# Spreading fourteen projection tiles over the Hyena transforms and moving the mLSTM branch behind them

## The chip, the cores and the metric

The kernel runs on one core of a Trainium2 chip. The metric is the device time of one execution in microseconds (us). The core's engines run their own instruction streams and wait for one another by semaphores: TensorE (PE) multiplies, ScalarE (ACT), VectorE (DVE) and GpSimd (POOL) work elementwise, and SyncE (SP) only issues transfers (DMA). The others issue transfers too, each in the queue of its own name.

## What is computed

One layer of a hybrid model: two token mixers side by side on the same normalised input, then a mixture of experts. 1,024 tokens (after 256 context tokens), width 1,024, fp32.

```
def token_mixer(h, w_in, b_in, ...):
    p = h @ w_in + b_in
    y_a = hyena_branch(p[..., :ML_START], ...)             # 3 x 512 columns
    y_b, state = mlstm_branch(p[..., ML_START:GATE_START], p[..., GATE_START:MERGE_START], ...)
    g_a, g_b = split(sigmoid(p[..., MERGE_START:]), 2)     # 2 x 1024 columns: the merge gates
    return (g_a * (y_a @ w_branch_hy) + g_b * (y_b @ w_branch_ml)) @ w_out, state

def hyena_branch(hy_p, ...):      # z <- x_n * (h_n conv z), twice, the convolution by FFT
    z = parts[0]
    for o in range(2):
        z = parts[o + 1] * bidir_long_conv(z, filt[:, o], skip[o])

def mlstm_branch(...):            # two scans over chunks of 128 tokens, one each way
    h = h2[:B] + flip(h2[B:])
    h = h * rsqrt(mean(h * h) + RMS_EPS) * norm_g          # per head
    return h * sigmoid(o)
```

After the mixers come a residual, a second norm, a router that lets each of 16 experts pick 128 tokens, the experts' SwiGLU, and the final norm.

## The kernel before

Every fp32 operand of a product is split in two parts (`split`: the high part `hi` by a cast on ACT, the low part `lo` by a subtraction on DVE or POOL), and a product is three matmuls (`mm3`: high by high, high by low, low by high). All engine calls go through one helper, so that the trace gives most instructions line 98; tiles are told apart by their names.

The stages, in order of time: the filters and the tokens' preparation with the first projections (to 336 us); the mLSTM stage (336 to 657 us); the head norm with more projection (657 to 797 us); the Hyena transforms (797 to 1008 us); the branch outputs, `w_out` and the router (to 1147 us); the choice of tokens (to 1212 us); the experts (to 2320 us).

**Projection.** `rest()` computes 32 tiles of 128 columns of `w_in` over all tokens (`hx`), each in two halves of 512 tokens of 24 matmuls: tiles j = 0 to 11 are Hyena's columns, 12 to 15 the mLSTM's output gate (to `o_d` in DRAM), 16 to 31 the merge gates (`gate_half`, a sigmoid, to `ga_d` and `gb_d` in DRAM). Weights come in blocks of 256 columns (`load_w`, `block`). A call of `rest_tile()` makes one tile in three substeps and, at its third, one step of `ada_rest` (the rest of the modulation, whose weights `wada` are loaded in blocks of 1 MB).

**mLSTM.** `mlstm()` runs two scans of ten chunks, forward and backward taking turns, each chunk (`ml_step`) in three substeps: 60 in all, one at each substep of 20 rest tiles. Within a step one chain goes through four engines: PE writes the log weights `pL` and the scores `pS`, ACT makes the exponentials `ae`, POOL masks them, DVE multiplies them by the scores (`ae<-ae,sc`), and PE needs the product for `pn<-v1c,ae`. The projection's matmuls (`ps<-hx,whi`, `ps<-hx,wlo`) stand between `pL` and `pn`.

**Head norm.** `head_norm()` norms the heads' outputs, transposes them on PE (`ps<-cst,hs`), multiplies by the output gate read from `o_d` and splits the result at once into `yb`, kept in SBUF. Eight more rest tiles stand between its parts, and the last four (`gate_tail`) behind them, with the loads of Hyena's tables (`hyena_pre`).

**Hyena.** There are four channel groups and two orders. `hyena_fwd(g, o)` has two steps (F = 0, 1): 24 matmuls `hyf<-D,hf` with 256 columns, then on DVE a chain `hX`, `hdf`, `hX`, `hY<-hX,Kt`, `hX<-hX,Kt`, `hY`, then on POOL `hY`, `hgd`, `hG`. The filters' spectra `Kt` are loaded from DRAM for each step, on SP's queue. `hyena_inv0` and `hyena_inv1` transform back, in fp32 (`hyE<-hG,hi`; with `hyE<-hi,hG` and `hyO<-hi,hG` for the second order). Between these steps `do` puts the units of `ml_branch`, the product of `yb` with `w_branch_ml` (`wmh`, `wml`): 16 units of 12 matmuls, each multiplied by a gate from `gb_d` (`mgb`). The last of all is `hyena_inv1(3)`, with the first half of four output products (`ps<-z,wb`) ahead of it.

**What sets the order.** A scheduler places the instructions of each engine, and on PE, ACT, DVE and POOL they need not stand in the order of the program. Small tiles of 2 KB a partition come from one pool of 12 buffers (`w2`); PSUM has eight banks.

Of the kernel before, what the change touches and what calls it, by code (L numbers as in the profile page):

```python
# [21 lines left out]
D = 1024  # L22
# [81 lines left out]
def layer_kernel(ctx: ExitStack, tc: tile.TileContext, A: dict, out: bass.AP, dbg=None, stop=None):  # L104
# [65 lines left out]
    o_d = dr.tile([512, 1024], F32, name="o_d")  # L170
    ga_d = dr.tile([1024, 1024], F32, name="ga_d")
# [509 lines left out]
    def to_chunks(dst_d, c0, j, cv, n_tok):  # L681
# [8 lines left out]
              + [[(3600 + 256 * b, 256)] for b in range(8)])  # L690
# [287 lines left out]

    def gate_half(w, j, n):
        dst, r0, c0 = (o_d, j - 12, c_bin + 24) if j < 16 else (ga_d, j - 16, c_bmg) if j < 24 else (gb_d, j - 24, c_bmg + 8)  # L980
        t = proj_half(w, j % 2, n * 512, col(c0 + r0))
        S.dma_start(dst[r0 * 128:(r0 + 1) * 128, n * 512:(n + 1) * 512], t)

    def rest():
        post = None
        for j in range(28):
# [63 lines left out]
    def rest_tile():  # L1050
        next(rs_)
        yield
        next(rs_)
        yield
        next(rs_, None)
        next(ar, None)
        yield


    yb = {}  # L1060

    def head_norm():
# [6 lines left out]
        yield  # L1069
        y0 = [al1([128, 4, 512], F32R, name="yb0", tag=t) for t in ("hch", "hcl")]  # L1070
        for n in range(2):
            pt = []
            for h in range(4):
                p = ps()
                for c in range(4):
                    T.transpose(p[:, c * 128:(c + 1) * 128], hsv(n * 4 + c)[:, h, :], ident)
                pt.append(p)
                if h % 2 == 1:
                    yield
            for h, p in enumerate(pt):  # L1080
                ot = w2([128, 512], name="ot")
                SY.dma_start(ot, o_d[h * 128:(h + 1) * 128, n * 512:(n + 1) * 512])
                V.scalar_tensor_tensor(ot, p, col(c_mng + h), ot, op0=OP.mult, op1=OP.mult)
                if n == 0:
                    hi, lo = y0[0][:, h], y0[1][:, h]
                else:
                    t = alx([128, 2, 512], F32R, name="yb1", tag="xt", bufs=4)
                    hi, lo = t[:, 0], t[:, 1]
                split(hi, lo, ot)
                yb[n, h] = hi, lo  # L1090
# [4 lines left out]
    for _ in range(20):  # L1095
        for _ in rest_tile():
            next(ml)
    if dbg is not None and "hs" in dbg:
        for i in range(4):
            SY.dma_start(dbg["hs"][:, 2 * i:2 * i + 2], hs[i])  # L1100
    hn = head_norm()
    for _ in range(8):
        for _ in rest_tile():
            next(hn, None)
    for _ in hn:
        pass
    for _ in ar:
        pass
    dump("eo", eo_d)
    mlp.close()  # L1110


    def gate_tail():
        for n in range(2):
            for j in range(28, 32):
                gate_half(block(6 + j // 2), j, n)
                yield
# [4 lines left out]
    n_D = [0]  # L1122

    def hyena_data():


        n_D[0] += 1
        al_, kw = (al, {"tag": "D2", "bufs": 2}) if n_D[0] % 3 == 0 else (alxl, {"tag": "xl", "bufs": 4})
        return tuple(al_([128, 4, 2, 128], F32R, name="D", **kw) for _ in range(2))
# [13 lines left out]
    def hyena_pre():  # L1143
        htab.append([al1([128, 2, 2, 4, 128], F32R, name=f"hf{v}", tag=f"hx0{v}", bufs=2) for v in range(2)])
        htab.append(al1([128, 2, 2, 4, 128], name="hi", tag="hx00", bufs=2))
        load_eo(0)
        for F in range(2):
            for c in range(2):
# [3 lines left out]
            if F == 0:  # L1152
                load_eo(1)
            yield
        SY.dma_start(htab[1], A["hi"])
# [17 lines left out]
    gt = gate_tail()  # L1173
    for _ in range(4):
        next(gt)
    run((hyena_pre(), 1), (gt, 1))
    p2.close()
    sx2.close()
    if stop == "mlstm":
        sxl.close()  # L1180
        sx1.close()
        sxt.close()
        return


    pz, p3 = ExitStack(), ExitStack()
    alz = phase(pz, "z")
    zs = {}
    al = phase(p3, "hyena")


    def ml_branch():
        ws = []

        def load():
            d_ = len(ws)
            raw = w2([128, 4, 128], name="wmr")
            S.dma_start(raw, A["w_branch_ml"][0][:, d_ * 128:(d_ + 1) * 128].rearrange("(k p) n -> p k n", p=128))
            w = [al([128, 4, 128], F32R, name=f"wm{v}", bufs=2) for v in "hl"]
            split(w[0], w[1], raw, G)  # L1200
# [3 lines left out]
        for d_, n in [(d_, n) for d_ in range(6) for n in range(2)] + [(d_, n) for n in range(2) for d_ in (6, 7)]:  # L1204
            yield
            if n == 0 and d_ < 7:
                load()
            sg = w2([128, 512], name="mgb")
            S.dma_start(sg, gb_d[d_ * 128:(d_ + 1) * 128, n * 512:(n + 1) * 512])
            p = ps()  # L1210
            for ct in range(4):
                mm3(p, [t[:, ct] for t in ws[d_]], yb[n, ct], ct == 0, ct == 3)
            V.tensor_tensor(sg, p, sg, op=OP.mult)
            SY.dma_start(mb_d[d_ * 128:(d_ + 1) * 128, n * 512:(n + 1) * 512], sg)
# [8 lines left out]
    def hyena_fwd(g, o):  # L1223
# [4 lines left out]
        if o == 0:  # L1228
            t = al([128, 4, 2, 128], name="hxe", tag="hx4", bufs=3)
            SY.dma_start(t.rearrange("p t x c -> p t (x c)"), eo_d[1, g].rearrange("t p x c -> p t (x c)"))  # L1230
        else:
            t = al([128, 1024], name="x2t", tag="hx4", bufs=3)
# [3 lines left out]
        for F in range(2):  # L1236
            Kt = al([128, 2, 2, 2, 128], name="Kt", bufs=3)
# [716 lines left out]
```

## Time and profile before

| what | us |
|---|---|
| median of three runs | 2340.99 (2339.63 to 2345.29) |
| the profiled execution, its own time | 2339.34 |
| its span in the profile | 2337.6 |
| PE busy in the span | 2183.2 |
| mLSTM stage, 336 to 657 | 321 |
| head norm, 657 to 797 | 140 |
| Hyena, 797 to 1008 | 211 |
| branch outputs, `w_out`, router, 1008 to 1147 | 139 |
| choice of tokens, 1147 to 1212 | 65 |
| experts, 1212 to 2320 | 1108 |

Read the stages first: an engine's busy time in a stage against the stage's length says which engine sets it. PE's clock is given as a share of full speed. Then come the waits of the engine that sets the stage, and last the instructions in order of time, where the length of a chain can be read off.

### The profile page before, as it was taken

The numbers are of one execution on the slowest core, as the hardware profiler recorded it, in microseconds if no ns is written. First come the engines' busy times: TensorE is split into PE (matmuls) and PEld (weight loads), VectorE is DVE, ScalarE is ACT, GpSimd is POOL, SyncE is SP. The second block draws the span as 40 slices with busy tenths as digits, with TensorE's granted clock in tenths as the row PEclk, the third lists the DMA queues.
The fourth block names the chain that finished last, engine by engine and source line by source line (L and its number), as shares of the span: only waits on it lengthen the run. The fifth ranks groups of instructions, "written<-read, shape, count | busy, mean of one in ns | idle before, by whom it ended". The sixth has DMA issues, their size and how long they took to land. (4 is left out here: it accounts for less than half of the span.)

```text
span 2337.6 us, 28219 instructions
## 1 busy us (share of the span) xinstructions
PE 2183.2 (93%) x10609; PEld 1777.0 (76%) x10609; DVE 1689.3 (72%) x1845; ACT 1244.1 (53%) x1388; POOL 447.2 (19%) x382
## 2 busy tenths in 40 slices
PE   6989999999999988799639999999999999999996
PEld 3679887787778777577538888888888888888884
DVE  4784445654341388963678889988898988888897
ACT  2441343334542211221427777787777777777774
POOL 3553101111100266532300110101111010111001
PEclk9879999999999989899869999999999999999998
DMA  7243335556533533384559999999999999999993
GB/s 260 91 139 91 120 113 164 202 171 216 171 113 101 159 112 125 113 265 167 184 213 367 384 382 379 389 385 377 387 385 380 379 391 381 379 389 382 380 348 147
DMA packets 227721, 600.97 MB, mean 257 GB/s; under 512 B 17307, under 2 KB 83927, under 8 KB 224385
## 3 DMA queue, kind: packets, MB, share of 16 engines
q1 hardware_dynamic: 203792, 543.05, 63.4%
q0 software_dynamic: 11488, 39.33, 5.4%
q10 hardware_dynamic: 12304, 16.80, 2.1%
q8 instruction: 83, 1.36, 0.2%
q14 instruction: 54, 0.43, 0.1%
HBM read 537.24 MB, written 61.88 MB: 256 GB/s over the span
## 5 line engine op out<-in xcount | busy, mean ns | idle before, releaser
L98 DVE TENSOR_TENSOR el<-er,eh 128x2048 fp32r<-128x2048 f32 x383 | 874.3, 2290 | 115.3 <-ACT eh L98 106.1
L98 ACT CAST eh<-er 128x2048 fp32r<-128x2048 f32 x384 | 733.6, 1915 | 236.8 <-PE pup L98 166.7
L98 PE MATMUL ps<-hx,whi 128*128 128x512 f32 x1280 | 404.5, 397 | 0.0
L98 PE MATMUL pup<-eh,xgh 128*128 128x512 f32 x1024 | 320.1, 394 | 1.6 <-ACT xgh L98 1.6
L98 PE MATMUL pup<-eh,xgl 128*128 128x512 f32 x1024 | 316.7, 390 | 0.0
L98 PEld LDWEIGHTS ps<-hx,whi 128*128 128x128 f32 x1280 | 237.9, 188 | 54.2 <-ACT nt L98 0.8
L98 PE MATMUL pup<-el,xgh 128*128 128x512 f32 x1024 | 274.3, 390 | 0.0
L98 PE MATMUL ps<-hx,wlo 128*128 128x512 f32 x640 | 252.5, 395 | 0.0
L98 PEld LDWEIGHTS pup<-eh,xgl 128*128 128x128 f32 x1024 | 192.9, 188 | 40.8 <-DVE xgl L98 0.2
L98 PEld LDWEIGHTS pup<-el,xgh 128*128 128x128 f32 x1024 | 192.5, 188 | 40.2
L98 PEld LDWEIGHTS pup<-eh,xgh 128*128 128x128 f32 x1024 | 190.4, 188 | 40.3 <-ACT xgh L98 2.0
L98 POOL DMA_INDIRECT acc_d<-ye,idxc x15 | 50.6, 3375 | 747.9 <-DVE ye L98 747.9
L98 PE MATMUL acc<-eh,gh 128*128 128x512 f32 x512 | 161.7, 397 | 0.2 <-ACT gh L98 0.2
L98 PE MATMUL acc<-eh,gl 128*128 128x512 f32 x512 | 160.3, 394 | 0.0
L98 PEld LDWEIGHTS ps<-hx,wlo 128*128 128x128 f32 x640 | 120.1, 188 | 28.2
L98 PE MATMUL acc<-el,gh 128*128 128x512 f32 x512 | 139.7, 394 | 0.0
L98 DVE TENSOR_TENSOR wlo<-wraw,whi 128x1024 fp32r<-128x1024 f32 (+1 forms) x44 | 55.8, 1271 | 100.4 <-ACT whi L98 93.8
L98 PEld LDWEIGHTS acc<-eh,gl 128*128 128x128 f32 x512 | 96.2, 188 | 22.8 <-DVE gl L98 0.4
L98 PEld LDWEIGHTS acc<-el,gh 128*128 128x128 f32 x512 | 96.1, 188 | 22.6
L98 PEld LDWEIGHTS acc<-eh,gh 128*128 128x128 f32 x512 | 95.0, 188 | 21.7 <-ACT gh L98 0.5
L98 ACT ACTIVATE pb<-ps,colv 128x512 f32<-128x512 f32 (+1 forms) x44 | 29.2, 665 | 130.1 <-PE ps L98 122.4
L98 ACT ACTIVATE sg<-ps,colv 128x512 f32<-128x512 f32 x40 | 27.5, 687 | 129.6 <-PE ps L98 123.2
(363 smaller groups left out, 3224.5 us busy)
## 6 DMA issues: line engine op xcount, KB each, us to landing
er<-in_w_exp_dram SPq DMA_DIRECT2D x384, 1024.0 KB
wada<-in_w_ada_dram SPq DMA_DIRECT2D x24, 1024.0 KB
wraw<-in_w_in_dram SPq DMA_DIRECT2D x40, 512.0 KB
K_d<-fk SPq DMA_DIRECT2D x32, 256.0 KB
Kt<-K_d SPq DMA_DIRECT2D x16, 512.0 KB
v1c<-v_d SPq DMA_DIRECT2D x20, 256.0 KB
eo_d<-eost POOLq DMA_DIRECT2D x16, 256.0 KB, 6.9
qc<-q_d SPq DMA_DIRECT2D x16, 256.0 KB
```

Of the source, the lines that this page charges most:

```text
L98: r = op(*a, **k)
```

## The change

- **Projection.** `rest()` stops after tile 17. The tiles j = 18 to 31 are made by a new generator `gate_tiles_T`: 28 steps, each half of the depth of one tile for all tokens (24 matmuls into a pair of PSUM banks `pg`), with weights `gwr` of 128 columns by 512 rows, loaded on SP's queue, cast on ACT (`gwh`), subtracted on DVE (`gwl`), three buffers each. `interleave` puts the 28 steps between 30 steps of Hyena.
- **mLSTM.** The same 60 substeps take 48 places of 16 rest tiles (`ml_steps`), and `ada_rest` does two of its steps per tile instead of one. The head norm has the last two rest tiles beside it, with the loads of Hyena's tables.
- **mLSTM output.** `head_norm` stores its product in `y_d` in DRAM (POOL's queue); `load_y` loads it again (`yr`) and splits it into `yb`. `ml_branch` stands behind the interleaved part, its units beside `hyena_inv1(2)` and `hyena_inv1(3)` and then beside `split_z` and the loads of `wb`. Its low part `wml` is made on DVE instead of POOL.
- **Hyena's buffers.** `Kt` has two instead of three, `hxe`/`x2t` two instead of three; `hY` gets two of its own (it shared four with `hX`); `hG` has none of its own, its values are written into `hX`. `z` is kept in fp32 (`z32`) and split later, and no output product starts before `hyena_inv1(3)`.

The core of the diff:

```diff
-              + [[(3600 + 256 * b, 256)] for b in range(8)])
+              + [[(3600, 256)]])
...
-        for j in range(28):
+        for j in range(18):
...
-        next(ar, None)
+        for _ in range(2):
+            next(ar, None)
...
+                V.scalar_tensor_tensor(ot, p, col(c_mng + h), ot, op0=OP.mult, op1=OP.mult)
+                G.dma_start(y_d[at], ot)
...
+    def ml_steps():
+        n = 0
+        for i in range(48):
+            yield
+            while n * 48 < (i + 1) * 60:
+                next(ml)
+                n += 1
...
+    def gate_tiles_T():
+        todo = [(j, kh) for j in range(18, 32) for kh in range(2)]
...
+            raw = w2([128, 4, 128], name="gwr")
+            SY.dma_start(raw, w_in[kh * 512:(kh + 1) * 512, c0:c0 + 128].rearrange("(k p) n -> p k n", p=128))
+            w = [alw([128, 4, 128], F32R, name=f"gw{v}", bufs=3) for v in "hl"]
+            split(w[0], w[1], raw)
             ws.append(w)
...
+        for i, (j, kh) in enumerate(todo):
             yield
-            if n == 0 and d_ < 7:
+            while len(ws) < min(i + 3, len(todo)):
                 load()
...
+            if kh == 0:
+                p = ps("pg"), ps("pg")
+            for k in range(4):
+                for n in range(2):
+                    mm3(p[n], [t[:, k] for t in ws[i]], hx(kh * 4 + k, n * 512, 512), kh == 0 and k == 0, kh == 1 and k == 3)
...
-            Kt = al([128, 2, 2, 2, 128], name="Kt", bufs=3)
+            Kt = al([128, 2, 2, 2, 128], name="Kt", bufs=2)
...
-            Y = al([128, 2, 2, 2, 128], name="hY", tag="hX", bufs=4)
+            Y = al([128, 2, 2, 2, 128], name="hY", bufs=2)
...
-            Gf = al([128, 2, 2, 2, 128], name="hG", bufs=4)
             for i, op in enumerate((OP.add, OP.subtract)):
-                G.tensor_tensor(Gf[:, i].rearrange("p a b c -> p a (b c)"), y0, gd, op=op)
-            hG[g, o].append(Gf)
+                G.tensor_tensor(X[:, i].rearrange("p a b c -> p a (b c)"), y0, gd, op=op)
+            hG[g, o].append(X)
...
+    gt = gate_tiles_T()
+    next(gt)
+    hy = steps_of(hyena_fwd(0, 0), hyena_fwd(1, 0), hyena_inv0(0), hyena_inv0(1), hyena_fwd(0, 1), 2, hyena_fwd(1, 1), 3,
+                  hyena_inv1(0), hyena_fwd(2, 0), hyena_inv1(1), hyena_fwd(3, 0), hyena_inv0(2), hyena_inv0(3),
+                  hyena_fwd(2, 1), hyena_fwd(3, 1))
+    interleave(gt, hy, 28, 30)
...
+    def load_y(n):
+        hi, lo = (al1([128, 4, 512], F32R, name="yb", tag=f"hx0{v}", bufs=2) for v in range(2))
+        for h in range(4):
+            t = w2([128, 512], name="yr")
+            SY.dma_start(t, y_d[h * 128:(h + 1) * 128, n * 512:(n + 1) * 512])
+            split(hi[:, h], lo[:, h], t)
+            yb[n, h] = hi[:, h], lo[:, h]
...
+    for _ in steps_of(hyena_inv1(2), hyena_inv1(3)):
+        next(mlj)
...
+    for ct in range(4):
+        load_wb(ct)
+        next(mlj)
+        split_z(ct)
+        next(mlj)
+    for _ in mlj:
```

What moves on the engines is shown at three places. On PE in the last quarter of the mLSTM stage: `pL` ends PE's part of the weights' chain, `pn` is the first that needs its end (`ae`), and rows `ps<-hx` are projection. Before:

```order
L98 MATMUL ps<-hx_932,whi 128x512
L98 MATMUL ps<-hx_934,whi 128x512
L98 MATMUL ps<-hx_932,wlo 128x512
L98 MATMUL pL<-rbd,onesr 128x512
L98 MATMUL ps<-hx_1271,whi 128x512
L98 MATMUL ps<-hx_1273,whi 128x512
L98 MATMUL ps<-hx_1271,wlo 128x512
```

After:

```order
L98 MATMUL ps<-hx_1275,whi 128x512
L98 MATMUL ps<-hx_1273,wlo 128x512
L98 MATMUL pL<-rbd,onesr 128x512
L98 MATMUL pn<-v1c,ae 128x129
L98 MATMUL pq<-Cst_4985,qc 128x129
```

Before, at least 24 projection matmuls stand behind each `pL` of the sixteen steps with an output; after, in four of the sixteen there is none, in two more six, and in the other ten 24 to 37.

On PE in the Hyena transforms, at one `hyena_inv0`. Before:

```order
L98 MATMUL ps<-yb_5997,wmh 128x512 x2
L98 MATMUL ps<-yb_5997,wml 128x512
L98 MATMUL hyE<-hG,hi 128x256 x16
L98 MATMUL ps<-yb_5790,wmh 128x512
```

After:

```order
L98 MATMUL pg<-hx_1273,gwh 128x512
L98 MATMUL pg<-hx_1275,gwh 128x512
L98 MATMUL pg<-hx_1273,gwl 128x512
L98 MATMUL hyE<-hX,hi 128x256 x8
L98 MATMUL pg<-hx_932,gwh 128x512
```

Where 12 matmuls with `yb` stood between whole transforms, 24 projection matmuls now stand between any two steps, strictly in turn from the second forward transform to the last.

On SP, which issues nearly all loads in one queue, the start of the Hyena transforms. Before:

```order
L1238 DMA Kt<-K_d 128x8x128 x2
L1230 DMA hxe<-eo_d 128x4x256
L1238 DMA Kt<-K_d 128x8x128 x2
L1230 DMA hxe<-eo_d 128x4x256
L1238 DMA Kt<-K_d 128x8x128
L1214 DMA mb_d<-mgb 128x512
```

After:

```order
L1224 DMA hxe<-eo_d 128x4x256
L1232 DMA Kt<-K_d 128x8x128
L1188 DMA gwr<-in_w_in_dram 128x4x128 x2
L1232 DMA Kt<-K_d 128x8x128
L1188 DMA gwr<-in_w_in_dram 128x4x128
L1232 DMA Kt<-K_d 128x8x128
L1188 DMA gwr<-in_w_in_dram 128x4x128
```

The weight slabs `gwr` now stand behind the loads of `Kt`, each of which waits for a buffer.

On DVE at the end of the Hyena transforms. Before:

```order
L98 TENSOR_TENSOR hY<-hX,Kt 128x512
L98 TENSOR_TENSOR z<-zt,z 128x512 x2
L98 TENSOR_TENSOR hY<-hX,Kt 128x512
L98 TENSOR_TENSOR hX<-hX,Kt 128x512 x2
L98 TENSOR_TENSOR hY<-hY,hX 128x512
L98 TENSOR_TENSOR mgb<-ps,mgb 128x512 x2
```

After:

```order
L98 TENSOR_TENSOR hX<-hX,Kt 128x512 x2
L98 TENSOR_TENSOR hY<-hY,hX 128x512
L98 TENSOR_TENSOR wml<-wmr,wmh 128x512
L98 TENSOR_TENSOR yb<-yr,yb 128x512 x4
L98 TENSOR_TENSOR wml<-wmr,wmh 128x512
L98 TENSOR_TENSOR yb<-yr,yb 128x512 x4
L98 TENSOR_TENSOR mgb<-ps,mgb 128x512
```

The low parts of `wm` and `yb`, which the first unit of `ml_branch` needs, stand behind the last forward chain.

## Rows read from the trace of the kernel before

**Rows 1.** Which stage is bound by what: busy time of the engines by stretch

```profile
core 0: us, PE busy (x) PEld busy (x) DVE busy (x) ACT busy (x) POOL busy (x), PEclk, DMA share, GB/s
...
336.00:657.00 321.00, 317.81 (x1697) 252.57 (x1696) 167.25 (x332) 127.25 (x269) 44.87 (x72) 1.00 0.55 181
657.00:797.00 140.00, 137.65 (x632) 112.36 (x631) 33.55 (x57) 37.26 (x59) 5.53 (x4) 1.00 0.32 106
797.00:1008.00 211.00, 168.86 (x855) 144.39 (x854) 181.29 (x233) 39.25 (x72) 115.42 (x100) 0.89 0.45 139
```

**Rows 2.** What PE waited for in the Hyena stretch, 797 to 1008 us

```profile
engine line waited for: us in total, times, longest us
PE hyE L98 <- POOL hG L98: 15.8, 4, 7.1
PE ps L98 <- DVE ga L98: 10.1, 2, 6.0
PE hyE L98 <- DVE mgb L98: 5.9, 1, 5.9
```

**Rows 3.** PE at 797 to 813 us in order: start, length, instruction

```profile
804.30 5.63 PE L98 MATMUL hyf<-D,hf 128*128 128x256 f32 x48
809.76 0.62 PE L98 MATMUL ps<-yb,wmh 128*128 128x512 f32 x2
...
812.51 0.81 PE L98 MATMUL hyE<-hG,hi 128*128 128x256 f32 x3
```

**Rows 4.** PE in order of time at 994 to 1003 us

```profile
995.76 3.61 PE L98 MATMUL hyE<-hi,hG 128*128 128x256 f32 x16
999.22 3.62 PE L98 MATMUL hyO<-hi,hG 128*128 128x256 f32 x16
```

**Rows 5.** Groups of instructions in the Hyena stretch: count, mean, idle

```profile
L98 PE MATMUL ps<-z,wb 128*128 128x512 f32 x44 | 13.4, 462 | 8.2 <-DVE wb L98 5.6 <-ACT wb L98 2.1 <-ACT z L98 0.5
```

**Rows 6.** ACT at 709 to 727 us: two gate halves, one after the other

```profile
714.58 0.69 ACT L98 ACTIVATE sg<-ps,colv 128x512 f32<-128x512 f32 x1 [4.90 <-PE ps L98]
...
720.17 0.69 ACT L98 ACTIVATE sg<-ps,colv 128x512 f32<-128x512 f32 x1 [4.90 <-PE ps L98]
```

**Rows 7.** DVE at 808 to 818 us: the forward chain of one step

```profile
809.13 0.68 DVE L98 TENSOR_TENSOR hX<-hyf,hsb 128x512 f32<-128x512 f32 x1
...
814.72 1.28 DVE L98 TENSOR_TENSOR hX<-hX,Kt 128x512 f32<-128x512 f32 x2
...
817.59 0.68 DVE L98 TENSOR_TENSOR hX<-hyf,hsb 128x512 f32<-128x512 f32 x1
```

**Rows 8.** All engines at 415 to 421 us: a chain of mLSTM

```profile
416.06 0.48 PE L98 MATMUL pL<-rbd,onesr 104*128 104x512 f32 x1
...
418.85 0.69 DVE L98 SCALAR_TENSOR_TENSOR ae<-ae,sc 128x512 f32<-128x512 f32 x1 [1.05 <-POOL ae L98]
```

**Rows 9.** All engines at 644 to 651 us: the last chain of mLSTM

```profile
644.46 0.40 PE L98 MATMUL pL<-rbd,onesr 104*128 104x512 f32 x1
...
645.37 1.28 ACT L98 ACT_TABLE_LOAD   x1
...
646.66 1.14 ACT L98 ACTIVATE ae<-pL,mcols 128x128 f32<-128x128 f32 x4
...
648.54 0.69 DVE L98 SCALAR_TENSOR_TENSOR ae<-ae,sc 128x512 f32<-128x512 f32 x1 [6.87 <-POOL ae L98]
```

**Rows 10.** ACT at 840 to 846 us: branch weights, issue and cast

```profile
840.93 0.39 ACTq L98 DMA_DIRECT2D wmr<-in_w_branch_ml_dram  x1
...
844.53 0.62 ACT L98 CAST wmh<-wmr 128x512 fp32r<-128x512 f32 x1 [0.79 <-DMA wmr<-in_w_branch_ml_dram]
```

**Rows 11.** ACT at 889 to 897 us: a later slab of the same size

```profile
889.77 0.39 ACTq L98 DMA_DIRECT2D wmr<-in_w_branch_ml_dram  x1
...
895.40 0.62 ACT L98 CAST wmh<-wmr 128x512 fp32r<-128x512 f32 x1 [2.76 <-DMA wmr<-in_w_branch_ml_dram]
```

**Rows 12.** PE at 655 to 668 us: the head norm's first transposes

```profile
666.15 0.66 PE L98 MATMUL ps<-cst,hs 128*128 128x128 f32 x4 [2.35 <-DVE hs L98]
```

More of the change, by code (lines that the diff above doesn't have):

```diff
@@ L1094, in layer_kernel @@
     ml = mlstm()
-    for _ in range(20):
-        for _ in rest_tile():
[L1097 to L1105, printed above, removed]
+    def ml_steps():
[5 more added lines that the diff above has]
+                n += 1
+    mls = ml_steps()
+    next(mls)
+    for _ in range(16):
+        for _ in rest_tile():
+            next(mls, None)
+    for _ in ml:
         pass
@@ L1151, in hyena_pre @@
                 split(htab[0][0][:, F, c], htab[0][1][:, F, c], raw)
[L1152 to L1155, printed above, removed]
+                yield
+    hn, hp = head_norm(), hyena_pre()
+    for _ in range(2):
+        for _ in rest_tile():
+            next(hn, None)
+            next(hp, None)
+    run((hn, 1), (hp, 1))
+    dump("eo", eo_d)
+    mlp.close()
     AB2 = late([128, 2, 8], F32, name="AB2")
@@ L1171, in layer_kernel @@
     V.tensor_copy(rb, p[:, 0:16])
[L1173 to L1176, printed above, removed]
     p2.close()
-    sx2.close()
     if stop == "mlstm":
+        sx2.close()
         sxl.close()
@@ L1314, in hyena_inv1 @@
         S.copy(es, pE[0])
-        zt = [w2([128, 512], name="zt") for _ in range(2)]
+        if g < 3:
+            z = alx([128, 2, 512], name="z32", tag="xt", bufs=4)
+            zt = [z[:, h] for h in range(2)]
+        else:
+            zt = [w2([128, 512], name="zt") for _ in range(2)]
         for n, op in ((1, OP.add), (0, OP.subtract)):
@@ L1327, in hyena_inv1, with steps_of, ml_branch, load @@
             hs_ = slice(h * 512, (h + 1) * 512)
[L1328 removed]
+            split(zs[g][0][:, hs_], zs[g][1][:, hs_], z32[g][h])
+    def steps_of(*gens):
+        for g in gens:
+            if isinstance(g, int):
+                load_eo(g)
+            else:
+                yield from g
+    gt = gate_tiles_T()
[4 more added lines that the diff above has]
+    interleave(gt, hy, 28, 30)
+    pgw.close()
+    sx2.close()
+    pwm = ExitStack()
+    alwm = phase(pwm, "wm", side="right")
+    yb = {}
+    def load_y(n):
[5 more added lines that the diff above has]
+            yb[n, h] = hi[:, h], lo[:, h]
+    def ml_branch():
+        ws = []
+        def load():
+            d_ = len(ws)
+            raw = w2([128, 4, 128], name="wmr")
+            S.dma_start(raw, A["w_branch_ml"][0][:, d_ * 128:(d_ + 1) * 128].rearrange("(k p) n -> p k n", p=128))
+            w = [alwm([128, 4, 128], F32R, name=f"wm{v}", bufs=2) for v in "hl"]
+            split(w[0], w[1], raw)
+            ws.append(w)
+        load()
+        load_y(0)
+        for d_, n in [(0, 0), (1, 0)] + [(d_, 1) for d_ in range(2)] + [(d_, n) for d_ in range(2, 8) for n in range(2)]:
+            yield
+            if (d_, n) == (0, 0):
+                load()
+                load_y(1)
+            elif n == 0 and 1 < d_ < 8 or (d_, n) == (1, 1):
+                if len(ws) < 8:
+                    load()
+            sg = w2([128, 512], name="mgb")
+            S.dma_start(sg, gb_d[d_ * 128:(d_ + 1) * 128, n * 512:(n + 1) * 512])
+            p = ps()
+            for ct in range(4):
+                mm3(p, [t[:, ct] for t in ws[d_]], yb[n, ct], ct == 0, ct == 3)
+            V.tensor_tensor(sg, p, sg, op=OP.mult)
+            SY.dma_start(mb_d[d_ * 128:(d_ + 1) * 128, n * 512:(n + 1) * 512], sg)
         yield
@@ L1442, in layer_kernel @@
     gate_tiles(0)
-    for i, p in enumerate(first):
-        for ct in (2, 3):
-            hy_mm(p, i, ct)
-        hy_out(p, i)
-    for i in range(4, 16):
+    for i in range(16):
         p = ps()
```

134 lines of the change are left out of this document (42 added, 92 removed).

## The prediction

> **What bounds the kernel now.** I read the stretches first, for the busy time of each engine in each stage. In the mLSTM stage PE is busy 317.81 of 321 us, in the head norm's 137.65 of 140, both at the full granted clock [rows 1]: nothing is to be had there but by taking matmuls away. In the Hyena stretch PE is busy 168.86 of 211 us, its granted clock is 0.89 of full, and DVE is busy 181.29 us [rows 1]. That stretch is the only one of the three with room. The waits say whom PE waited for there: POOL's `hG`, 15.8 us in four waits, DVE's `ga`, 10.1 us in two, and DVE's `mgb` once for 5.9 us [rows 2]. Each of these ends a forward or an inverse step on DVE and POOL, for which PE had only 12 matmuls with `yb` to fill the time.
>
> How much of the 211 us is not matmul work at full pace? The timeline gives the paces. 48 `hyf` matmuls take from 804.30 to 809.76, 0.114 us each; 12 with `yb` take from 809.76 to 812.51, 0.229 each [rows 3]; 16 records of an fp32 inverse take from 995.76 to 999.22, 0.216 each [rows 4]. The stretch holds 384 `hyf` less the 27 that start before 797, 256 records of inverses (8 of 32), 192 with `yb` and 44 with `z` [rows 5]: 40.7 + 55.3 + 44.0 + 10.1 = 150.1 us. So 211 - 150.1 = 60.9 us are lost: 42 are idle (211 less 168.86 busy), and the other 19 are matmuls that ran at the lower of the clock's two levels, 1.2 instead of 2.4 GHz.
>
> **What the change moves.** The number of matmuls stays. 28 half tiles leave the well filled stages and come between the Hyena steps. Two gate halves in a row end 5.59 us apart, at 714.58 and 720.17 [rows 6], so the steps carry 28 x 5.59 = 156.5 us into the stretch. The 16 units with `yb` (44.0 us) go behind it. Before, PE had 2.75 us of other work between two Hyena steps, now it has 5.59. Against the chain of a forward step on DVE, 8.46 us from 809.13 to 817.59 [rows 7], PE then has 24 `hyf` and 24 `pg`, 2.74 + 5.59 = 8.3 us, about as much. PE, and no longer DVE, becomes the engine with the most work there, and the 60.9 us are what can be recovered in full. From this come new losses.
>
> **(a) The denser mLSTM stage.** 60 substeps now lie in 48 places, and the order shows that of sixteen steps with an output four have no projection matmul between `pL` and `pn`, and two have six. That cover hid a chain. From `pL` at 416.06 to the end of `ae<-ae,sc` at 418.85 + 0.69 it takes 3.5 us [rows 8]; in the last chain, from 644.46 to 648.54 + 0.69, it takes 4.8, of which 1.28 is the load of an activation table on ACT [rows 9]. Six matmuls cover 1.4 us: 2 x 2.0 = 4. Of the four without cover I place two in each pass: 2 x 3.2 and 2 x 4.5 (less 0.3 for `pL` itself) = 15.4. Sum 19.4. Around such waits the clock may fall, and `wada`, 1 MB each, is now loaded twice per tile instead of once; I add 6 us for both, an estimate from the Hyena stretch, where 42 us of idle went with 19 of lost clock [rows 1]. Taken: 25.5, with 12 (part of the chains are done earlier, while PE still works off what stands ahead of `pL`; DVE idles 6.87 us ahead of `ae<-ae,sc` [rows 9]) to 40 as bounds. Nothing below: the stage idles only 3.2 us now [rows 1].
>
> Behind the table load of 1.28 us, `ae` starts within 0.01 us of its end (645.37 + 1.28, 646.66) [rows 9]. The Trainium skill ("ScalarE: Activation LUTs", What ACT_TABLE_LOAD costs) counts another 1,380 ns of drain to every switch of tables, 2.66 us in all. This trace shows no such gap behind the load at this place, and the row decides; by the page the two uncovered steps of the second pass would each be 1.4 us longer and the forecast 2330.
>
> **(b) New waits in the Hyena stretch.** The weights of a half tile, a slab of 256 KB, are issued on SP behind `Kt`, and `Kt` now has two buffers. A `Kt` buffer comes free when the last product with it ends, at 814.72 + 1.28, 6.9 us after its chain began [rows 7]. Only then does SP pass on. A slab of the same shape took 3.6 us from its issue at 840.93 to the start of its cast at 844.53 [rows 10], later, with other loads ahead, 5.6 (889.77 to 895.40) [rows 11]. I take 4.0, near the first, because SP then has at most one other load in flight. With an issue before it (0.5), cast (0.62) [rows 10] and subtraction (0.69, as another 128x512 operation of DVE [rows 8]) the slab is ready 6.9 + 0.5 + 4.0 + 0.6 + 0.7 = 12.7 us after a chain's start. PE's own work until it asks, two half tiles and one `hyf` step, is 2 x 5.59 + 2.74 = 13.9. So in the regular place the slab is just in time; at the start and at three places where a shorter piece stands in the row, I get 1.7, 2.0, 2.0 and 0.3 = 6 us, with the clock 8. Bounds: 0, and 8 + 26 = 34 (second rival). The store of the head norm's output and its reload lie on POOL's and SP's queues beside PE's work and cost nothing unless SP is late anyway.
>
> **(c) The tail.** At the end DVE has the low parts `wml` and `yb` behind the last forward chains. In the order four such chains, 4 x 8.46 = 33.8 us, and then seven operations of 0.69 (4.8), with about 2 us for the last inverse's evictions, must end before the first product with `yb`: DVE arrives 40.5 us after the first of these chains begins. PE's own work up to there is 2 `hyf` steps, 4 half tiles and 8 fp32 matmuls (16 records): 5.5 + 22.4 + 3.5 = 31.2 us. PE waits 9.3 us, with the clock 12. From 5 (scheduler's order as it is, but one chain already done) to 20.
>
> **(d) The head norm.** Before, PE waits 2.35 us for DVE's `hs` [rows 12]. Now two tiles instead of eight stand beside it, and one more such wait is possible: +1, from 0 to 5.
>
> **Sum.** 60.9 - (25.5 + 8 + 12 + 1) = 14.4 us gained. Against the profiled execution, 2339.34: 2324.9. The median of the runs is 1.65 above it, so 2327.
>
> **Rivals.** *All of it hides* (0.14): the scheduler's order lets the chains of (a) run while PE still has earlier matmuls queued, and slabs come early. Then 43 of the 60.9 come home (17.5 lost, the low ends of (a) and (c) and about nothing else): 2298. For it speaks that DVE is far from full in the mLSTM stage (167.25 of 321 [rows 1]); against it, that `pn` stands directly behind `pL` in the order.
>
> *The slabs become the bound* (0.20), which ends slower. Place: PE at the first `pg` matmul of a half tile, waiting for `gwl`. Price: if a slab lands in 5.6 instead of 4.0 us [rows 11], each of the 16 steps behind a forward chain starts 1.6 us later and nothing makes it up, as the next `Kt` waits for the same chain: 26 us, 2353. It decides from about the landing of 5.2 us on, where 12.7 + 1.2 reaches PE's 13.9. For it speaks that `Kt` (512 KB) always lands just ahead; against it, that the core's DMA share in the stretch is only 0.45 [rows 1]. The Trainium skill ("Perfetto Trace Analysis", Optimization Strategy) reads the same gap repeating on the engine that should be saturated as a sign that there may not be enough memory for the next tile, and buffers are just what this change cuts. In the trace of before, PE's waits in this stretch are for DVE and POOL, none for a load of `Kt` [rows 2]; no run yet shows the case with two buffers.
>
> *mLSTM's chain becomes the bound of its stage* (0.18): not six but all sixteen steps wait, each what a step with six matmuls pays, 3.5 - 1.4 to 4.8 - 1.4, say 2.5. 40 us in place of 25.5: the losses are 61, and the time is 2341, no change. For it: 60 substeps in 48 places. Against it: ten of the sixteen keep 24 matmuls or more.
>
> *The half tiles are not spread* (0.03), if the scheduler drew them together: 2341. The order of the changed kernel shows them strictly in turn, so this is nearly excluded.
>
> **How the numbers follow.** Forecast 0.45 at 2327, its own range 2314 to 2338. The range for 8 in 10 takes in part of both sides: 2304 to 2358. About 0.3% (7 us) is what a measurement of this kernel can tell from no change. Faster by more: 0.40 of the forecast's 0.45 and the first rival's 0.14, 0.54. Within: 0.05 of the forecast, 0.12 of the mLSTM rival and the 0.03, 0.20. Slower: the slabs' 0.20 and 0.06 of the mLSTM rival, 0.26.
>
> **What would show it.** Right: in the Hyena stretch of after PE is at least 0.95 busy at a clock near full; in the mLSTM stage there are six waits of PE for `ae`, 2 to 5 us each; at the end one wait of about 9 us for `yb` or `wml`. The slab rival shows as many waits for `gwl` or `gwh`, and as DVE's or ACT's idle ended by a load of `gwr`. The mLSTM rival shows as waits for `ae` or `hs` at all sixteen steps. I would be wrong if PE's clock stayed below 0.95 in the new stretch although the waits are gone, if PE waited for PSUM (`pg`) because ACT's sigmoids stand behind Hyena's copies, or if the stages behind, from the router on, changed at all.

## The result: slower by 0.8 %, and where the time went

The changed kernel takes 2357.06 us (median of five runs, 2355.51 to 2368.44) against 2340.99 (2339.34 to 2345.29): 1.0079 of the time before, with a 95 % interval of 1.0053 to 1.0104. The forecast was 2327, so the sign was wrong. The profiled execution spans 2355.3 us, 17.7 more than before.

Up to 336 us both kernels do the same work to within two matmuls. From there the program is cut at three events that both have: PE's first `hyf`, the last product with `z`, and the experts' first matmul. The stretches of the profile, first of the kernel before, then of the changed one (length, busy time and count of each engine, PE's granted clock, DMA share, GB/s):

```profile
336.00:794.40 458.40, 452.86 (x2304) 362.33 (x2303) 200.81 (x388) 163.82 (x327) 50.40 (x76) 1.00 0.48 158
794.40:1042.30 247.90, 205.76 (x1025) 174.69 (x1024) 204.72 (x265) 50.52 (x91) 132.85 (x114) 0.91 0.50 154
1042.30:1207.70 165.40, 109.10 (x601) 84.49 (x599) 93.34 (x236) 43.01 (x86) 43.12 (x51) 0.84 0.53 194
```

```profile
336.00:694.00 358.00, 310.54 (x1629) 249.76 (x1627) 179.34 (x365) 118.12 (x271) 58.43 (x83) 0.95 0.50 169
694.00:1054.50 360.50, 347.98 (x1698) 294.35 (x1698) 211.58 (x304) 88.73 (x151) 118.63 (x102) 0.98 0.46 147
1054.50:1224.90 170.40, 111.96 (x601) 86.42 (x599) 99.02 (x243) 44.43 (x88) 47.14 (x54) 0.83 0.54 196
```

The 14 moved tiles are estimated at 156.5 us of PE work (28 x 5.59 [rows 6]). With them counted where they now stand:

| stretch | before | after | after, like for like | difference |
|---|---|---|---|---|
| 336 us to the first `hyf` | 458.4 | 358.0 | 358.0 + 156.5 = 514.5 | +56.1 |
| to the last `ps<-z` | 247.9 | 360.5 | 360.5 - 156.5 = 204.0 | -43.9 |
| to the experts' first matmul | 165.4 | 170.4 | 170.4 | +5.0 |
| the experts | | | | +0.5 |

The sum is the measured 17.7. In the Hyena part the change did what it should: PE is busy 347.98 of 360.50 us there, at a clock of 0.98 instead of 0.91. The loss lies ahead of it. PE was idle 5.5 us from 336 us to the first `hyf`; now it is idle 47.5 us, and its clock is 0.95. What PE waited for there (in all, times, longest):

```profile
PE pn L98 <- DVE ae L98: 28.0, 7, 5.3
PE pL L98 <- POOL rbd L98: 5.5, 2, 3.8
PE ps L98 <- DVE hs L98: 3.1, 2, 2.2
PE ps L98 <- DMA wr<-in_w_router_dram: 3.0, 1, 3.0
PE pk L98 <- DMA kt<-k_d: 2.7, 1, 2.7
```

`ae` is the end of the weights' chain of an mLSTM step: PE's `pL`, then ACT, POOL, DVE, then `pn` on PE. Six of the seven waits are at the six steps that have no projection matmul between `pL` and `pn`, called bare from here on; they make 26.0 us. Two of them in order of time, all engines of the changed kernel (start, length, instruction, idle before):

```profile
449.72 0.48 PE L98 MATMUL pL<-rbd,onesr 104*128 104x512 f32 x1
...
450.48 1.15 ACT L98 ACTIVATE ae<-pL,mcols 128x128 f32<-128x128 f32 x4
...
451.70 1.24 POOL L98 TENSOR_SCALAR_AFFINE_SELECT ae<-ae 128x512 f32<-128x512 f32 x1 [0.79 <-ACT ae L98]
...
453.41 2.13 DVE L98 TENSOR_TENSOR eo<-cv 128x512 f32<-128x512 f32 x3
...
455.46 0.68 DVE L98 SCALAR_TENSOR_TENSOR ae<-ae,sc 128x512 f32<-128x512 f32 x1
...
456.20 0.80 PE L98 MATMUL pn<-v1c,ae 128*128 128x129 f32 x2 [4.12 <-DVE ae L98]
```

```profile
615.75 1.05 ACT L98 CAST whi<-wraw 128x1024 fp32r<-128x1024 f32 x1 [1.73 <-PE ps L98]
615.78 0.40 PE L98 MATMUL pL<-rbd,onesr 104*128 104x512 f32 x1
616.70 0.68 ACT L98 ACTIVATE sg<-ps,colv 128x512 f32<-128x512 f32 x1
617.40 1.28 ACT L98 ACT_TABLE_LOAD   x1
...
618.69 1.14 ACT L98 ACTIVATE ae<-pL,mcols 128x128 f32<-128x128 f32 x4
...
620.58 0.69 DVE L98 SCALAR_TENSOR_TENSOR ae<-ae,sc 128x512 f32<-128x512 f32 x1 [2.53 <-POOL v1c L98]
...
621.33 0.80 PE L98 MATMUL pn<-v1c,ae 128*128 128x129 f32 x2 [5.14 <-DVE ae L98]
```

From the start of `pL` to the end of `ae<-ae,sc` it takes 6.4 and 5.5 us, where the prediction read 3.5 and 4.8 [rows 8, 9]. In the first, POOL is done at 452.94, but DVE has the rest tile's convolution part (`eo<-cv`) ahead of `ae<-ae,sc`. In the second, ACT first casts the weights of a later tile (`whi`), then does the tile's sigmoid (`sg`) and a table load; the last two stand in the chain of [rows 9] as well. The seventh wait is of another kind: a step with its full 24 matmuls, whose chain took longer than they do,

```profile
593.37 0.49 PE L98 MATMUL pn<-v1c,ae 128*128 128x129 f32 x2 [1.95 <-DVE ae L98]
```

Where do bare steps come from? A rest tile offers three places for substeps: before its first 24 matmuls, between the halves, and behind the second. Between the third place and the next tile's first there are no projection matmuls at all. As long as a tile takes exactly one step, the step's second substep (`pL`) falls between the halves and its third (`pn`) behind the second, with 24 matmuls between. With 60 substeps in 48 places the steps slide against the tiles. By the arithmetic of `ml_steps`, of the sixteen steps with an output three have `pL` behind a tile and `pn` ahead of the next, and three have both in the one place behind a tile. In these six nothing is between them, and the tile's own work on ACT and DVE can be in the way. The trace has the same six: no projection matmul in six steps, 24 in each of the other ten. (The order had shown four bare steps and two with six matmuls; in the trace PE has in those two only the scores `pS` and the modulation's `ada`.) The two waits for `rbd`, which the first substep makes, are at steps whose first substep stands behind a tile and whose second ahead of the next. That was the theory to test. Its rivals: the density itself (the chain no longer fits beside the work), the loads, and the other parts of the change.

### The profile page after: what moved, and what is told of

Same layout as the page of the kernel before. It is cut to its first block, busy times and chain, and to the rows that moved or that the text cites. A ratio compares the mean times of both kernels' runs of the same rounds, so it can differ in the third digit from the quotient of the medians.

```text
span 2355.3 us, 28306 instructions
## 1 busy us (share of the span) xinstructions
PE 2186.7 (93%) x10609; PEld 1787.6 (76%) x10609; DVE 1681.0 (71%) x1867; ACT 1238.1 (53%) x1394; POOL 445.2 (19%) x382
## 5 line engine op out<-in xcount | busy, mean ns | idle before, releaser
L98 PE MATMUL ps<-hx,whi 128*128 128x512 f32 x832 | 265.5, 400 | 0.0
L98 PEld LDWEIGHTS pup<-eh,xgl 128*128 128x128 f32 x1024 | 192.8, 188 | 40.9 <-DVE xgl L98 0.2
L98 PEld LDWEIGHTS ps<-hx,whi 128*128 128x128 f32 x832 | 155.4, 190 | 34.1
L98 PE MATMUL ps<-hx,wlo 128*128 128x512 f32 x416 | 164.8, 396 | 0.0
L98 PE MATMUL pg<-hx,gwh 128*128 128x512 f32 x448 | 141.9, 399 | 2.6 <-ACT gwh L98 2.6
L98 PEld LDWEIGHTS pg<-hx,gwh 128*128 128x128 f32 x448 | 83.7, 189 | 20.5 <-ACT gwh L98 2.8
L98 POOL DMA_INDIRECT xg<-xn_d,idxc x16 | 44.9, 2804 | 259.4 <-PE ps L98 226.3
```

The source lines that it names most:

```text
L98: r = op(*a, **k)
```

## The experiments

**The pace alone.** The kernel before with the new pace of the substeps and two steps of `ada_rest` per tile; the four tiles left over go beside the head norm:

```diff
-    for _ in range(20):
+    mls = ml_steps()                       # as in the change
+    next(mls)
+    for _ in range(16):
         for _ in rest_tile():
-            next(ml)
+            next(mls, None)
...
-        next(ar, None)
+        for _ in range(2):
+            next(ar, None)
...
-    for _ in range(8):
+    for _ in range(12):
         for _ in rest_tile():
             next(hn, None)
```

> The kernel before with only the pace of the change: 60 substeps in 48 places of 16 rest tiles and two steps of ada_rest per tile; the four tiles that are left follow beside the head norm; all else is before. Theory (the pace alone costs what the mLSTM stage lost): 40 to 54 us over before, 2380 to 2395 us, with PE's waits for ae near 28 us. Rival (the loss needs the rest of the change, by shorter buffers or other loads): at most 20 us over before, 2345 to 2360 us.

2390.56 us (2385.61 to 2395.73), 1.0205 of before (1.0185 to 1.0225), 50 us more. PE's two largest waits from 336 to 850 us:

```profile
PE pn L98 <- DVE ae L98: 28.0, 7, 5.3
PE pL L98 <- POOL rbd L98: 5.5, 2, 3.8
```

They are those of the changed kernel to the tenth, and the stretch up to the first `hyf` (at 848.3) is 53.9 us longer than before. So the loss of the mLSTM stage comes with the pace and the denser `ada_rest` alone (the latter is taken out below); the buffers, the output through DRAM and Hyena are not needed for it.

**The place alone, made worse.** The kernel before with its own density, but two substeps run ahead, so that every `pL` stands behind a tile and its `pn` ahead of the next:

```diff
+    for _ in range(2):
+        next(ml)
     for _ in range(20):
         for _ in rest_tile():
-            next(ml)
+            next(ml, None)
```

> The kernel before, with the same 60 substeps beside the same 20 rest tiles, but two substeps run ahead of the first tile, so that in all sixteen steps the second substep stands at the end of a tile and the third at the start of the next: in the order no projection matmul stands between pL and pn any more, while density, loads and buffers are those of before. Theory (the place): each of the sixteen waits for ae costs 4 to 5.5 us as the seven in the changed kernel did, 65 to 90 us in all with the clock: 2400 to 2430 us. Rival (the density made it): nothing changes, 2335 to 2350 us.

2429.33 us (2426.68 to 2434.28), 1.0388 of before (1.0363 to 1.0412), 90 us more from two substeps. PE's waits and the stretch up to the first `hyf`:

```profile
PE pn L98 <- DVE ae L98: 62.1, 16, 6.0
```

```profile
336.00:882.30 546.30, 481.53 (x2292) 393.12 (x2291) 197.71 (x384) 160.43 (x322) 53.45 (x75) 0.93 0.40 131
```

All sixteen steps are bare and wait, 3.9 us each. Density, loads and buffers are unchanged; the place is enough. The stretch grew by 87.9 us and its idle time by 59.3 (64.8 less 5.5): each idle us went with half another of slower matmuls, at a granted clock of 0.93.

**The place alone, mended.** The changed kernel at its own density, with the substeps placed by hand so that every `pL` has 24 projection matmuls or more before its `pn`:

```diff
+        at = [i if i < 4 else 4 + (i - 3) * 26 // 16 for i in range(20)]
+        where = [w for i in range(20) for w in (at[i - 1] + 1 if i else 0, at[i], at[i] + 1)]
         n = 0
         for i in range(48):
             yield
-            while n * 48 < (i + 1) * 60:
+            while n < 60 and where[n] <= 2 * (i // 3) + i % 3 - 1:
                 next(ml)
                 n += 1
```

> The changed kernel at the same density (60 substeps beside 16 rest tiles, two steps of ada_rest per tile), with the substeps placed so that in the order all sixteen pL have at least 24 projection matmuls before their pn; a step's first and second substep, with its loads, stand in one place in some steps instead. Theory (the place: where a step's second substep fell at the end of a rest tile and its third at the start of the next, nothing stood between them): PE's waits for ae before pn, 28 us in seven, fall under 5 us, and the time to about 2330 us. Rival (the density: mLSTM's chain is longer than the work beside it, wherever the cover stands): those waits go, but PE waits as long for kt, qc and rbd before pk, pS and pL; 2350 to 2360 us.

2311.35 us (2306.12 to 2320.25), 0.9879 of before (0.9847 to 0.9911): 46 us less than the changed kernel, at the same density. The stretch up to the first `hyf`, and all PE's waits in it:

```profile
336.00:649.00 313.00, 297.61 (x1620) 237.28 (x1618) 174.78 (x364) 116.66 (x269) 58.60 (x84) 0.98 0.57 192
```

```profile
PE ada L98 <- DMA wada<-in_w_ada_dram: 6.7, 3, 3.3
PE ps L98 <- DVE hs L98: 3.6, 3, 2.2
PE pk L98 <- DMA kt<-k_d: 3.1, 3, 2.2
PE pS L98 <- DMA qc<-q_d: 1.2, 2, 0.6
PE ps L98 <- DMA wr<-in_w_router_dram: 0.7, 1, 0.7
```

All sixteen steps have their 24 matmuls. The waits for `ae` and for `rbd` are gone, and the clock is back at 0.98. Of the 56.1 us, 11.3 remain (the first `hyf` is at 649.2: 313.2 + 156.5 - 458.4), mostly in waits for loads. The three other kernels below that have this stretch unchanged leave 9.2, 12.2 and 17.3, so this rest is known to within some us only. The density may have its part in it, as the rival said, but so may the tiles missing from the head norm and the places of the loads; no run separates them. The time fell further than expected, since the waits for `rbd` and the lost clock went with those for `ae`.

**The pace of before.** 20 tiles for mLSTM, `ada_rest` once per tile, two tiles beside the head norm, only ten spread:

```diff
-        for j in range(18):
+        for j in range(22):
...
-    for _ in range(16):                    # and 60 places instead of 48
+    for _ in range(20):
...
-        todo = [(j, kh) for j in range(18, 32) for kh in range(2)]
+        todo = [(j, kh) for j in range(22, 32) for kh in range(2)]
...
-    interleave(gt, hy, 28, 30)
+    interleave(gt, hy, 20, 30)
```

> The changed kernel with the mLSTM pace of before: 60 substeps in 60 places of 20 rest tiles, one step of ada_rest per tile, two more rest tiles beside the head norm; only ten tiles (20 half tiles) are spread over the 30 Hyena steps. By PE's starts against each matmul's usual pace, the changed kernel loses 85 us from 336 us to its first hyf, the kernel before 31 us in the same work; everything from there to the last ps<-z loses 19 us after and 61 before. Theory (the pace of mLSTM's substeps is what went wrong): the first loss falls to about 35 us, 50 less; with 20 instead of 28 half tiles the Hyena part loses up to 15 us more; 2310 to 2325 us. Rival (Hyena needs all 28 half tiles): the first loss falls as well, but 30 of the 42 us won in Hyena go again; about 2340 us. Rival (the loss lies in the shorter buffers or the output through DRAM, not the pace): no better than 2350 us.

2312.07 us (2306.40 to 2320.86), 0.9886 of before (0.9854 to 0.9918). By the table's reckoning the first stretch loses 2.3 us against before (348.9 + 111.8 - 458.4) and the Hyena part wins 36.7 (323.0 - 111.8 = 211.2, for 247.9), so ten tiles carry most of what 14 do.

**The loads.** The changed kernel and then the aligned one with `ada_rest` once per tile (the edit is the one line of the change, undone):

> The changed kernel with one step of ada_rest per tile instead of two, so that the 1 MB loads of wada come half as densely on SP's queue; nothing else changed. Theory (the loads are a side cost): PE's waits for kt, qc, kw and wada in the first half of the mLSTM stage, about 10 us in the changed kernel, fall under 3, the waits for ae stay at 20 us or more; 2345 to 2350 us. Rival (the load queue behind wada is the main cause, the chain's inputs come late): the waits for ae and rbd fall too, below 12 us together; 2320 to 2330 us. Rival (no matter): 2355 to 2360 us.

2358.07 us (2350.89 to 2361.97): no difference to 2357, as its second rival said. PE's waits from 336 us on moved among themselves (46.2 us idle up to the first `hyf`, for 47.3), and the six bare steps still wait for `ae`:

```profile
PE pn L98 <- DVE ae L98: 23.3, 6, 4.7
PE pk L98 <- DMA kt<-k_d: 6.5, 2, 3.9
PE pL L98 <- POOL rbd L98: 4.6, 2, 2.9
```

> The aligned kernel with one step of ada_rest per tile. In the aligned kernel PE still waits 8.0 us for wada, 4.0 for kt and 1.7 for qc in the mLSTM stage. Theory (these are the loads crowding on SP's queue): they fall under 5 together, and the time by about 8 to 2300 to 2305 us. Rival (as in the changed kernel with one step per tile, nothing comes of it): 2308 to 2315 us.

2318.34 us (2309.06 to 2321.73), 0.9904 of before (0.9884 to 0.9924). That can't be told from the aligned kernel's 0.9879, and the 8 us expected were not won. The wait for `wada` did not fall: 10.8 us in three. Halving the 1 MB loads of a tile did not help; why these three come late stays open.

**The lead of the weights in the Hyena part.** The second rival of the prediction, the slabs as the bound, had no wait of its own in the changed kernel except at the second slab and one other. To see whether its mechanism exists, the aligned kernel got one buffer less, and with it each slab's load one half tile later:

```diff
-            w = [alw([128, 4, 128], F32R, name=f"gw{v}", bufs=3) for v in "hl"]
+            w = [alw([128, 4, 128], F32R, name=f"gw{v}", bufs=2) for v in "hl"]
...
-            while len(ws) < min(i + 3, len(todo)):
+            while len(ws) < min(i + 2, len(todo)):
```

> The aligned kernel with two instead of three buffers for the weights of a half tile, and the slab after next loaded one half tile later. In the changed kernel 24 of the 28 slabs are ready 2 to 15 us before PE asks for them and four arrive with it (by the starts of gwl on DVE and of each half tile's first pg). Theory (the spread works because of this lead; the rival on the slabs was right in its mechanism, the margin is only there with three buffers): without one half tile of lead, 8 us, about half of the steps wait 2 to 5 us, 30 to 60 us in all, 2340 to 2370 us. Rival (the loads have room anyway): 2306 to 2320 us.

2345.32 us (2339.08 to 2351.74), 34 us more than the aligned kernel. PE's waits from 640 to 935 us:

```profile
PE pg L98 <- ACT gwh L98: 27.2, 12, 4.1
```

In the same stretch ACT's casts `gwh` waited for the load of `gwr` thirteen times; they do in the changed kernel too, but there mostly ahead of PE's need. So the mechanism exists, and the third buffer with its half tile of lead holds it off.

**The tail.** PE's wait ahead of the first products with `yb` is 9.5 us in the changed kernel. In the aligned kernel with `ada_rest` once per tile, the loads of the first half were written ahead of the last forward transform and its low part given to POOL; then, with `ada_rest` twice per tile, the first `wml` went to POOL as well:

```diff
-            SY.dma_start(t, y_d[h * 128:(h + 1) * 128, n * 512:(n + 1) * 512])
-            split(hi[:, h], lo[:, h], t)
+            split(hi[:, h], lo[:, h], yrs[n, h], V if n else G)   # loaded by load_yr, ahead of hyena_fwd(3, 1)
...
-            split(w[0], w[1], raw)
+            split(w[0], w[1], raw, V if ws else G)                # the second of the two kernels only
```

> The aligned kernel with one step of ada_rest per tile, and with the loads of the first half of the mLSTM output written ahead of the last forward Hyena transform and its low part made on POOL instead of DVE. Theory of the tail (PE waits at the first product with yb because the low part stands behind the last forward chains on DVE, and the high part's loads were late): the wait of 9.5 us in the changed kernel falls under 4, 5 us less than without this edit. Rival (POOL's subtractions, 1.44 us each, now hold up POOL's part of the last forward chain, and PE waits for hX at the last inverse instead): no difference.

> The aligned kernel with the early loads and POOL's low part of the first half of the mLSTM output, and now the first low part wml on POOL as well (it stood behind the last forward chain on DVE, and PE waited 8.7 us for it). Theory: PE's waits ahead of and in the first unit with yb, 10.9 us in the aligned kernels and 12.1 with only the outputs moved, fall under 5; 5 us less than the aligned kernel's 2311. Rival (PE now waits for POOL, either for these low parts or for hX of the last inverse): within 2 us of 2311.

2317.53 us (2313.88 to 2326.69), for 2318.34 of its base, and 2320.58 (2318.66 to 2324.47), for 2311.35: nothing won, and in the second probably some lost, where the rival had said within 2 us. Both bases wait 9.4 to 9.7 us for `yb`. Around these products PE waits in the first, from 880 to 960 us,

```profile
PE ps L98 <- DVE wml L98: 8.4, 1, 8.4
PE ps L98 <- ACT wmh L98: 3.2, 1, 3.2
```

and in the second

```profile
PE ps L98 <- POOL wml L98: 15.0, 1, 15.0
PE ps L98 <- ACT wmh L98: 3.5, 1, 3.5
```

On either engine the last small piece stands behind a forward chain. The rival of the second run, a wait for POOL, holds as a mechanism; the wait was moved and grew, to 11.6 and 18.5 us.

**The output products.** The 5.0 us behind Hyena had not been forecast. All of it arises up to the last product with `w_out`, 110.1 us behind the last with `z` for 105.1; from there to the experts' first matmul it is 60.3 us in both kernels. Where PE waits there (1050 to 1080 us of the changed kernel, 1.2 and 0.5 us before):

```profile
PE ps L98 <- ACT woA L98: 3.1, 1, 3.1
PE ps L98 <- DVE woA L98: 0.9, 1, 0.9
```

Sixteen evictions `gab<-ps` on DVE are 3.97 us apart on average (1013.0 to 1072.6), before 2.63. DVE takes them one by one in turn with the low parts `mg`:

```profile
1043.54 0.69 DVE L98 TENSOR_TENSOR mg<-gab,mg 128x512 fp32r<-128x512 f32 x1 [2.11 <-ACT mg L98]
1044.14 0.68 DVE L98 TENSOR_TENSOR gab<-ps,gab 128x512 f32<-128x512 f32 x1
1046.95 0.69 DVE L98 TENSOR_TENSOR mg<-gab,mg 128x512 fp32r<-128x512 f32 x1 [2.12 <-ACT mg L98]
```

Two experiments: the odd low parts on POOL (aligned, `ada_rest` once per tile), and the products two at a time in a fixed order (aligned), as the kernel before has them.

```diff
-        split(mg[n][0][:, d_], mg[n][1][:, d_], ga)
+        split(mg[n][0][:, d_], mg[n][1][:, d_], ga, G if i % 2 else V)
```

```diff
+    in_order[0] = True
-    for i in range(16):
-        p = ps()
+    for i in range(0, 16, 2):
+        pd = ps(), ps()
...
+        hy_outs(pd, i)                     # both evictions, both sums, both splits, one load_wo
```

> The aligned kernel with one step of ada_rest per tile, and with the low parts mg of the odd output products made on POOL instead of DVE. In the changed kernel DVE takes the evictions gab<-ps,gab and the low parts mg one by one in turn, each through POOL and ACT, 3.45 us a product where PE needs 2.76, and PE then waits for woA for 4 to 5 us. Theory (this turn of DVE is the cause): the output products are evicted in 2.8 us each, and the time falls by 4 to 5 us against the same kernel without this edit. Rival (POOL becomes the bound with 1.4 us for each add and subtraction): no difference or 2 us more.

> The aligned kernel with the output products taken two at a time and the elementwise work behind them held in the order written: two evictions, two low parts, one woA on DVE, as the kernel before has it. Making the low parts on POOL did not help, as DVE's eviction then stood behind woA instead, whose cast stands behind mg on ACT. Theory (DVE's turn of one eviction and one low part, each through POOL and ACT, sets 3.9 us a product instead of 2.6): evictions are 2.6 to 2.8 us apart, PE's waits for woA fall from 4 to 5 us to about 2, and the time by 4 to 5 us from the aligned kernel's 2311. Rival (the loads of gab set the pace): the evictions stay 3.9 us apart and nothing is won.

The first, 2315.15 us (2312.44 to 2318.84), can't be told from its base (2318.34) and leaves the evictions 4.04 us apart: DVE's next eviction then stands behind `woA`, which waits for ACT. The second, 2313.56 us (2309.01 to 2313.90), brings them to 2.49 us, two at a time:

```profile
987.39 1.28 DVE L98 TENSOR_TENSOR gab<-ps,gab 128x512 f32<-128x512 f32 x2
990.14 1.94 DVE L98 TENSOR_TENSOR mg<-gab,mg 128x512 fp32r<-128x512 f32 x2 [1.46 <-ACT mg L98]
991.99 0.68 DVE L98 TENSOR_TENSOR woA<-wor,woA 128x512 fp32r<-128x512 f32 x1
```

But against the aligned kernel's 2311.35 the time does not fall, and PE still waits 3.7 us for `woA`; the theory held for the evictions alone. The turn on DVE sets the pace of the evictions; it is not what PE waits for. What makes the last `woA` late stays open.

**Between the two kernels.** Substeps aligned beside 18 tiles, two tiles beside the head norm, twelve spread, `ada_rest` once per tile, the output products two at a time:

> Between the changed kernel and the one before: mLSTM's substeps aligned beside 18 rest tiles with one step of ada_rest per tile, two more rest tiles beside the head norm, twelve tiles (24 half tiles) spread over the Hyena transforms, and the output products two at a time in the order written. Theory: the mLSTM part loses about 35 us as with 20 tiles, the Hyena part about 21 as with 28 half tiles, and the output products 4 less: 2300 to 2306 us, less than either kernel. Rival (the last few us of loss only move): 2308 to 2315 us.

2304.52 us (2301.85 to 2307.13), 0.9854 of before (0.9828 to 0.9880): faster than both kernels, and the lowest median of all runs here, though its interval overlaps those of four others, the aligned kernel among them. It changes several things at once and shows no single cause. Its stretches up to the first `hyf` and on to the last `ps<-z`:

```profile
336.00:660.00 324.00, 317.45 (x1718) 253.86 (x1716) 177.86 (x366) 126.75 (x279) 58.85 (x84) 0.99 0.59 194
660.00:1003.10 343.10, 326.78 (x1602) 276.66 (x1602) 222.15 (x307) 85.51 (x146) 122.50 (x106) 0.97 0.47 151
```

Like for like (twelve tiles, 134.2 us) the first costs what it cost before (324.1 + 134.2 = 458.3, for 458.4), and the second wins 39.1 us. The last stretch is 1.9 us longer than before.

## Why the prediction was wrong, step by step

- **What can be won in the Hyena stretch** (60.9 us, less 8 and 12 of new loss): right. The sum gave 40.9 us; 43.9 were measured. PE is 0.965 busy there, at a clock of 0.98, as the prediction's sign asked.
- **(b) The slabs**, 8 us: an upper value, in the right place. PE's waits of the changed kernel from 694 to 1055 us:

```profile
PE ps L98 <- ACT yb L98: 5.6, 1, 5.6
PE ps L98 <- DVE yb L98: 3.9, 2, 3.4
PE pg L98 <- ACT gwh L98: 2.6, 1, 2.6
PE pg L98 <- DVE gwl L98: 0.5, 1, 0.5
```

  Only the second slab and one other make PE wait; the rest come in time. The margin of about 1 us between 12.7 and 13.9 was too pessimistic for most of them: from the start of `gwl` to the half tile's first `pg` 24 of 28 have 2.7 to 15.5 us. The kernel with two buffers shows where it ends. The Trainium skill ("Perfetto Trace Analysis", Optimization Strategy) says that the same gap repeating on the engine that should be saturated can mean too little memory for the next tile. The traces agree on the repeating, though the gaps are not equal: twelve of 0.6 to 4.1 us, 27.2 in all, with two buffers, and two, 3.1 in all, with three.
- **(c) The tail**: 9.5 us of waiting for 9.3, and the size is partly luck, as the reason was half right. PE waits 5.6 us for `yb` from ACT, whose cast waits for the loads `yr` (issued from 939.21 us, cast at 948.83), and only then 3.9 for DVE.
- **(d) The head norm**: right by its wait. PE waits 3.1 us for `hs`, 0.7 more than before, for 1 forecast.
- **(a) The denser mLSTM stage**: this step failed, and it alone turns the sign. With (d) it was put at 26.5 us and measured 56.1. The mechanism was named and the six steps are the ones that waited, but its two terms were too small. The chain's term, 19.4, measured 28.0: the four steps without cover took 18.6 us for 15.4; the two that were given six matmuls of cover had none of projection and took 7.4 for 4.0; and a covered step waited 1.95. The chain had been read off where DVE was free ahead of `ae<-ae,sc` [rows 8, 9], while in the bare steps the tile's convolution on DVE or a cast on ACT can stand ahead of it. The other term, 6 us for loads and clock, was the larger miss: the other waits came to 13.9 us more than before (`rbd` 5.5, `wr` 3.0, `kt` 2.7, `wada` 2.0 and smaller ones, with 0.7 for `hs`), and the slower matmuls at the clock of 0.95 to 14.1. The prediction's own ratio, 19 of lost clock for 42 of idle, would have covered the clock, had the idle time of 42 us been foreseen. The bounds of (a) were 12 and 40; the measured value lies outside.
- **The table load** in a bare step: at 617.40 us it takes 1.28 us and `ae` starts 0.01 us behind its end, as in [rows 9]. The Trainium skill ("ScalarE: Activation LUTs", What ACT_TABLE_LOAD costs) counts a drain of 1,380 ns on top; no gap of that kind shows here either, and the measurement decides.
- **The stages behind**: assumed unchanged. Behind the products with `w_out` they are, but for the 0.5 us of the experts. The output products ahead of it cost 5.0 us more; the cause is narrowed down and not settled.
- **The rivals.** The mLSTM rival came nearest: the right stage, and a price of 40 us that was still under the 56. But it had all sixteen steps waiting because the chain is the bound. Six waited because of their place, and a seventh a little. At the same density and with the place mended, none of the sixteen waits for `ae`. The slab rival ended near the measured time (2353) by a mechanism that was not at work; that the range for 8 in 10 still takes in 2357 owes something to this rival's price, and is luck.

## What to carry to other kernels

When a side chain is spread over a main stream by a ratio, look at which seam of the main stream each of its links falls on. Filler that is plentiful on average covers nothing at a seam without work, and the chain can be slower just there, because the tile that ended has its own work queued on the same engines. Price a lost cover where it will be lost, and place the links by hand. Whole steps per tile only keep the place that the first one has: the kernel before has every link well placed, and two substeps' shift puts all sixteen wrong.

## What the runs showed of the hardware

Idle time on PE in short pieces went with a lower granted clock and cost more than itself. With 59.3 us of added idle, in waits of 2.6 to 6.0 us, the stretch grew by 87.9 us, at a granted clock of 0.93 (1.00 before); with 42, by 56.1 at 0.95. Mending the place brought the clock back to 0.98. So a wait of 4 us of PE was worth between 5 and 6 here. The idle sum alone does not fix the price: the changed kernel with `ada_rest` once per tile has 41 us of added idle, a clock of 0.92, and 61 us of loss.
